# 1/rms of three norms on VectorE, by Newton steps from a guess, in place of GpSimd's power

## The chip, the cores and the metric

The program runs on one core of a Trainium2 chip. Times are device microseconds of one execution, from runs of the whole program; profile times count from the start of the profiled span. Five engines work side by side, each through its own queue in order: TensorE (PE, with its weight loads PEld), VectorE (DVE), ScalarE (ACT), GpSimd (POOL) and SyncE (SP, which issues most DMAs). They meet only at semaphores.

## The reference, cut to what matters

One decoder layer, 1024 tokens by 1024 features, all in fp32: two attention branches with gates, a SwiGLU block with 2816 hidden features, a gated embedding term, and a last norm. The norms the change touches are the last three:

```python
def rms_norm(x, g):
    x32 = x.astype(jnp.float32)
    y = x32 * lax.rsqrt(jnp.mean(x32 * x32, axis=-1, keepdims=True) + EPS)
    return (y * g.astype(jnp.float32)).astype(x.dtype)
...
        n2 = rms_norm(h, g_ffn[i])
        h = h + (jax.nn.silu(n2 @ w_ffn_gate[i]) * (n2 @ w_ffn_up[i])) @ w_ffn_down[i]

        e = rms_norm(p[i] @ w_ple_proj[i], g_ple[i])
        h = h + jax.nn.sigmoid(h @ w_ple_gate[i]) * e
    return rms_norm(h, g_final)
```

Each norm needs 1/sqrt(mean square + eps) for every token, 1024 numbers per norm.

## The kernel before

Activations are held transposed: features on the 128 partitions, tokens along the free axis, in halves of 512 tokens (hf). Every matmul is made of three passes (lines 135 to 137, function passes): a factor is split into a high part, rounded by a ScalarE copy (L129), and a low part, a VectorE subtraction (L130, function split); PE then adds high by high (L135), high by low (L136) and low by high (L137). In PE's queue these lie in just this order, so L137 is the first to need the low part of the weight factor.

A sum over features is a sum over partitions. For a norm the squares are added up in a tile acc, and PE multiplies that by a column of ones (L166, L903, L1287) into a few columns of a PSUM tile pm: one number per token, tokens on the partitions, 128 to a column. rstd_finish takes it from there: VectorE adds eps (L170), GpSimd raises to the power -0.5 (L171). It is called eight times:

- for the embedding's norm from embed(0) and embed(1), 4 columns each, into r_ple, which is read only near the end of the program;
- for the FFN's norm from scales (through rstd_cols), for the first half of the tokens (4 columns), then for two quarters (2 columns each), into r_ffn;
- for the last norm, 4, 2 and 2 columns, into a tile r.

To multiply by such a number along the free axis it has to be spread over partitions: spread puts the columns on diagonals (L761, VectorE, `acc<-ident,cols`), and PE multiplies by ones (L764, tile bc). Then VectorE scales the activations by bc: `normed` (L875) for the FFN's norm, L1292 for the last.

Where the FFN begins, the program writes out several things that overlap. out_group adds the branch output to the residual, a feature block at a time (PE tiles po, L933, squares L935 and L938, sums L939). embed multiplies the 256 embedding features by w_ple_proj (PE tiles pp) and stores its results to d_e (L913). The FFN itself is a Strassen-Winograd product: seven products instead of eight over 2x2 blocks. Its right factors are b1 to b7 (Bn in the code, `right`), sums of normed activation blocks: b1 and b2 need only the first half of the tokens, b5 and b6 quarter after quarter of the second half (t1_factors, t2_factors), and b7, b3 and b4 all of it (L1095 to L1101). Its left factors come from weights (raw), partly through sums on GpSimd (s1 at L989, L990, L1006, L1008), split into tiles wl. PE adds the products into PSUM tiles pP, pQ, pR. FIRST gives the order of the products for the first three units: b1 and b2 for all three, then b5, b6, b7, b3, b4.

In the program's text the order is: out_group and scales of the first half, normed, b1 and b2; out_group, scales and t1_factors of the third quarter; out_group of the last quarter; embed(0); embed(1); then the first two products of three units; then scales of the last quarter (the third call from scales), its factors, and the rest. A scheduler in the framework takes this text, estimates when each instruction could run, and writes each engine's queue in that order, honouring all data dependences and given priorities (scales has high_priority 800). The queue is then fixed.

Tiles with one tag share buffers. Tag wl has three: the acc tiles of out_group, the embedding's e tiles and the first weight factors wl all come from these three. A buffer is free when its last reader is done; for acc that is the L764 matmul, for e the column sums and the store to d_e.

cols is one tile of 64 columns on all partitions, with constants, gains, r_ple (32 to 39) and r_ffn (40 to 47).

Of the kernel before, what the change touches and what calls it, by code (L numbers as in the profile page):

```python
# [12 lines left out]
I32 = mybir.dt.int32  # L13
AF = mybir.ActivationFunctionType
ALU = mybir.AluOpType
# [4 lines left out]
P = 128  # L20
# [5 lines left out]
EPS = 1e-6  # L26
# [25 lines left out]
def decoder_layer(ctx: ExitStack, tc: tile.TileContext, x, p, positions, g_mix, w_in, g_q_a, w_q_b,  # L52
                  g_kv_a, w_kv_b, w_br_mla, w_br_sb, w_out, g_ffn, w_ffn_gate, w_ffn_up, w_ffn_down,
                  w_ple_gate, w_ple_proj, g_ple, g_final, xT, pT, out):
    nc = tc.nc
# [50 lines left out]
    cols = const.tile([P, 64], F32, name="cols")  # L106
    mhalf = cols[:, 0:1]
# [47 lines left out]
    with ExitStack() as att:  # L155
# [6 lines left out]
        def rstd_cols(acc, out_r, n=4):  # L162

            pt = ps.tile([P, HALF], F32, name="pm", **M)
            for i in range(n):
                nc.tensor.matmul(pt[:, i:i + 1], lhsT=acc[:, i * P:(i + 1) * P], rhs=ones, start=True, stop=True)  # L166
            rstd_finish(pt, out_r, n)

        def rstd_finish(pt, out_r, n=4):
            nc.vector.tensor_scalar(out=out_r, in0=pt[:, 0:n], scalar1=EPS, scalar2=None, op0=ALU.add)  # L170
            nc.gpsimd.tensor_tensor(out=out_r, in0=out_r, in1=mhalf.broadcast_to([P, n]), op=ALU.pow)  # L171

        with ExitStack() as sb:
            nx = ExitStack()
# [108 lines left out]
            with ExitStack() as p2:  # L283
# [21 lines left out]
                V = nc.vector  # L305
# [174 lines left out]
            for pr in range(HEADS // 2):  # L480
                kst, q1, q2 = cur
                oT = wp.tile([P, S], F32, name="oT", tag="oT", bufs=1)
                for a in range(2):
# [5 lines left out]
                                            op=ALU.subtract)  # L489
# [28 lines left out]
        with ExitStack() as ml:  # L518
# [30 lines left out]
            for c in range(2):  # L549
                nc.vector.scalar_tensor_tensor(out=cn[c], in0=cn[c], scalar=gcol[:, 3 + c:4 + c], in1=rs,  # L550
                                               op0=ALU.mult, op1=ALU.mult)
# [32 lines left out]
            for c in range(3):  # L584
                t = wk.tile([P, S], F32, name="cq", tag="pw1", bufs=4)
                with tc.issue_after(fence[0]):
# [3 lines left out]
                                               op0=ALU.mult, op1=ALU.subtract)  # L590
# [306 lines left out]
    def embed(hf):  # L897
        pt = ps.tile([P, HALF], F32, name="pm", **B)
        es = []

        def column_sums(f):
            for i in range(4):
                nc.tensor.matmul(pt[:, i:i + 1], lhsT=es[f][:, 1, i * P:(i + 1) * P], rhs=ones, start=f + i == 0,  # L903
                                 stop=f == 7, skip_group_check=True)

        for f in range(NK):
            fs = slice(f * P, (f + 1) * P)
            pp = ps.tile([P, HALF], F32, name="pp", **A)
            passes(pp, [((wpj[:, 0, k, fs], wpj[:, 1, k, fs]), (pw[hf][:, 0, k, :], pw[hf][:, 1, k, :])) for k in range(2)])
            e = wk.tile([P, 2, HALF], F32, name="e", tag="wl", bufs=3)  # L910
            nc.scalar.copy(out=e[:, 0, :], in_=pp)
            nc.scalar.activation(out=e[:, 1, :], in_=pp, func=AF.Square, scale=1.0 / 32.0)
            nc.sync.dma_start(out=d_e[fs, hcol(hf)], in_=e[:, 0, :])  # L913
            es.append(e)
            if f:
                column_sums(f - 1)
        column_sums(7)
        rstd_finish(pt, r_ple[:, 4 * hf:4 * hf + 4])
# [267 lines left out]
    for i in (1, 2, 6, 5, 7, 3, 4):  # L1186
# [31 lines left out]
        f, t = {1: (0, 0), 2: (0, 0), 6: (0, 1), 5: (1, 1), 7: (1, 1), 3: (0, 1), 4: (1, 0)}[i]  # L1218
# [23 lines left out]
    for hf, c0, n in ((1, 0, 4), (0, 0, 2), (0, 2, 2)):  # L1242
# [4 lines left out]
        if hf == 0 and en is None:  # L1247
# [5 lines left out]
            for f in range(NK):  # L1253
                nc.vector.scalar_tensor_tensor(out=en[:, f, :], in0=en[:, f, :], scalar=gains[:, 1, f:f + 1], in1=bc[0],
                                               op0=ALU.mult, op1=ALU.mult)
        for f in range(NK):
# [5 lines left out]
            if hf:  # L1262
# [3 lines left out]
                                               op0=ALU.mult, op1=ALU.mult)  # L1266
# [17 lines left out]
        pt = ps.tile([P, HALF], F32, name="pm", **M)  # L1284
        for sq in (acc[:, 0, :], sg):
            for i in range(n):
                nc.tensor.matmul(pt[:, i:i + 1], lhsT=sq[:, i * P:(i + 1) * P], rhs=ones, start=sq is not sg and i == 0,  # L1287
                                 stop=sq is sg, skip_group_check=True)
        rstd_finish(pt, r[:, 0:n], n)
        bo = spread(acc[:, 1, :], r[:, 0:n], n, B)[:, w_]  # L1290
        for f in range(NK):
            nc.vector.scalar_tensor_tensor(out=hres[:, f, s], in0=hres[:, f, s], scalar=gains[:, 2, f:f + 1], in1=bo,  # L1292
                                           op0=ALU.mult, op1=ALU.mult)
# [39 lines left out]
```

## Time and profile before

| what | value |
|---|---|
| time, three runs | 1746.61, 1748.95, 1750.78 us; median 1748.95 |
| the profiled execution | 1749.03 us, span 1747.2 us |
| busy, share of span | PE 95%, DVE 64%, ACT 50%, POOL 21% |
| calls of the power (L171) | 5 between 939.4 and 998.2 us, 3 between 1693.1 and 1737.8 us |
| embedding's products on PE | first at 950.05 us |
| first FFN product on PE | 992.95 us |

Rows of a timeline read: start in us, duration in us, engine, line, operation, tile written <- tiles read, shapes, and in brackets how long the engine was idle before and what released it. "x8" merges eight instructions that follow each other. Where merged rows of two instructions start closer than the first lasts, their ends overlap. In rows of a chain stand only start, duration and what. In a table of stretches the engines' busy times stand in the order the header names. Buffer numbers are left out of tile names in the profile.

### The profile page before, as it was taken

What the parts mean: (1) busy time and instruction counts of PE and PEld (TensorE: products, weight loads), DVE (VectorE), ACT (ScalarE), POOL (GpSimd) and SP (SyncE); (2) the same over time, 40 slices, a digit from 0 to 9 for tenths busy, and PEclk for the clock granted to TensorE, in tenths of its full rate; (3) what the DMA queues carried; (4) which work ended last, traced back from release to release, by engine and by line L of the source; (5) the groups of instructions that cost most, each with busy time, mean ns of one, the idle gap of its engine ahead of it and who ended that gap; (6) DMA issues with size and microseconds to landing.
All of it is one profiled execution on the core that took longest, in us unless ns stands there. A gap on an engine that the chain in (4) does not pass through costs nothing.

```text
span 1747.2 us, 22835 instructions
## 1 busy us (share of the span) xinstructions
PE 1665.0 (95%) x8100; PEld 1383.4 (79%) x8100; DVE 1115.2 (64%) x1874; ACT 881.3 (50%) x1740; POOL 368.6 (21%) x389
## 2 busy tenths in 40 slices
PE   6999999999987999998999899999999999999997
PEld 5887778777776788886789787877778778888787
DVE  6655785576766777686568745565666545656665
ACT  5255676576675776686325633333333334445412
POOL 2012220000021333331001733344344310000000
PEclk9999999999998999999999999999999999999998
DMA  5221222212223322124854423364564528665522
GB/s 175 59 69 37 61 57 65 67 60 67 85 85 127 104 68 86 59 70 157 284 201 153 145 78 129 126 216 151 187 197 163 199 88 316 193 193 183 170 81 74
DMA packets 167987, 222.10 MB, mean 127 GB/s; under 512 B 22914, under 2 KB 97666, under 8 KB 167874
## 3 DMA queue, kind: packets, MB, share of 16 engines
q1 hardware_dynamic: 161298, 200.21, 35.6%
q0 software_dynamic: 6032, 19.93, 3.3%
q8 instruction: 63, 1.03, 0.2%
q10 hardware_dynamic: 544, 0.52, 0.1%
q14 instruction: 50, 0.41, 0.1%
HBM read 151.93 MB, written 67.90 MB: 126 GB/s over the span
## 4 chain that ended last, share of the span: by engine, by line
PE 74%; DVE 10%; issue 6%; ACT 4%; DMA 3%; POOL 3%; SPq 0%; POOLq 0%; DVEq 0%; ACTq 0%
PE pt L135 5%; PE pt L136 4%; PE pt L137 4%; PE pd L135 4%; PE pd L136 4%; PE pd L137 4%; PE pP L137 4%; PE pP L135 4%; PE pP L136 4%; PE pg L135 2%; PE pg L136 2%; PE pg L137 2%; PE pb L135 2%; DVE T L433 2%; PE pb L137 2%
## 5 line engine op out<-in xcount | busy, mean ns | idle before, releaser
L135 PE MATMUL pt<-nTh,w_h 128*128 128x512 f32 (+1 forms) x480 | 191.7, 405 | 1.6 <-DVE e L436 1.1
L137 PE MATMUL pt<-nTh,w_l 128*128 128x512 f32 (+1 forms) x480 | 189.7, 401 | 1.6 <-DVE w_l L130 1.6
L136 PE MATMUL pt<-nTl,w_h 128*128 128x512 f32 (+1 forms) x480 | 190.8, 402 | 0.0
L130 DVE TENSOR_TENSOR wl<-raw,wl 128x512 fp32r<-128x512 f32 x132 | 109.4, 830 | 102.5 <-ACT wl L129 101.9
L129 ACT CAST wl<-raw 128x512 fp32r<-128x512 f32 x132 | 82.0, 622 | 127.6 <-PE pP L137 54.5
L137 PE MATMUL pP<-b,wl 128*128 128x512 f32 x352 | 137.2, 392 | 9.0 <-DVE wl L130 9.0
L135 PE MATMUL pP<-b,wl 128*128 128x512 f32 x352 | 138.0, 392 | 5.0 <-ACT wl L129 4.5
L136 PE MATMUL pP<-b,wl 128*128 128x512 f32 x352 | 137.7, 391 | 0.0
L135 PEld LDWEIGHTS pt<-nTh,w_h 128*128 128x128 f32 (+1 forms) x480 | 91.6, 191 | 22.5 <-DVE e L436 1.9
L137 PEld LDWEIGHTS pt<-nTh,w_l 128*128 128x128 f32 (+1 forms) x480 | 91.3, 190 | 20.9 <-DVE w_l L130 2.0
L136 PEld LDWEIGHTS pt<-nTl,w_h 128*128 128x128 f32 (+1 forms) x480 | 91.3, 190 | 18.4
L136 PE MATMUL pd<-drs,dls 128*128 128x512 f32 x296 | 101.4, 389 | 0.0
L137 PE MATMUL pd<-drs,dls 128*128 128x512 f32 x296 | 101.2, 389 | 0.0
L130 DVE TENSOR_TENSOR drs<-drr,drs 128x512 fp32r<-128x512 f32 x74 | 50.9, 690 | 75.3 <-ACT drs L129 75.3
L135 PE MATMUL pd<-drs,dls 128*128 128x512 f32 x296 | 98.7, 392 | 0.0
L129 ACT CAST drs<-drr 128x512 fp32r<-128x512 f32 x74 | 45.9, 623 | 99.5 <-PE pd L137 93.3
L430 DVE SCALAR_TENSOR_TENSOR e<-z,e 128x128 f32<-128x128 f32 (+3 forms) x96 | 51.2, 550 | 60.5 <-ACT e L429 60.2
L657 POOL TENSOR_SCALAR pw<-pw,st 128x128 f32<-128x128 f32 (+5 forms) x48 | 74.1, 1548 | 74.3 <-PE sp L639 22.3
L137 PEld LDWEIGHTS pP<-b,wl 128*128 128x128 f32 x352 | 66.2, 188 | 26.0 <-DVE wl L130 12.4
L455 DVE TENSOR_TENSOR tl<-tp,th 128x512 fp32r<-128x512 f32 (+1 forms) x96 | 50.9, 549 | 51.5 <-ACT th L454 51.4
L135 PEld LDWEIGHTS pP<-b,wl 128*128 128x128 f32 x352 | 66.5, 189 | 19.2 <-ACT wl L129 4.8
L136 PEld LDWEIGHTS pP<-b,wl 128*128 128x128 f32 x352 | 66.5, 189 | 13.9
(368 smaller groups left out, 4596.6 us busy)
## 6 DMA issues: line engine op xcount, KB each, us to landing
d_g<-t SPq DMA_DIRECT2D x74, 256.0 KB, 2.7
drr<-d_g SPq DMA_DIRECT2D x74, 256.0 KB, 3.1
w_raw<-w_in SPq DMA_DIRECT2D x33, 512.0 KB, 4.0
raw<-w_ffn_gate SPq DMA_DIRECT2D x11, 1024.0 KB, 6.3
raw<-w_ffn_up SPq DMA_DIRECT2D x11, 1024.0 KB, 6.0
spare<-w_ffn_down SPq DMA_DIRECT2D x44, 256.0 KB, 3.7
d_w<-spare SPq DMA_DIRECT2D x44, 256.0 KB, 6.1
drr<-d_w SPq DMA_DIRECT2D x44, 256.0 KB, 2.6
```

Of the source, the lines that this page charges most:

```text
L129: nc.scalar.copy(out=h, in_=src)
L130: eng.tensor_tensor(out=l, in0=src, in1=r32(h), op=ALU.subtract)
L135: nc.tensor.matmul(ps, lhsT=ah, rhs=bh, start=first and i == 0, stop=False, **kw)
L136: nc.tensor.matmul(ps, lhsT=ah, rhs=bl, start=False, stop=False, **kw)
L137: nc.tensor.matmul(ps, lhsT=al, rhs=bh, start=False, stop=last and i == n - 1, **kw)
L430: nc.vector.scalar_tensor_tensor(out=e[:, 0:w], in0=z[:, 0:w], scalar=0.0, in1=e[:, 0:w], op0=ALU.max, op1=ALU.add)
L433: nc.vector.tensor_tensor_scan(out=T[:, 0:w][:, ::-1], data0=back, data1=back, initial=carry, op0=ALU.add, op1=ALU.max)
L455: nc.vector.tensor_tensor(out=tl[:, c0:], in0=tp[:, c0:], in1=r32(th[:, c0:]), op=ALU.subtract)
L657: nc.gpsimd.tensor_scalar(out=pw[:, 0:nk], in0=pw[:, 0:nk], scalar1=st[:, 6:7], scalar2=None, op0=ALU.mult)
```

## The change

rstd_finish no longer uses GpSimd. VectorE adds eps into a scratch column group m, shifts the bits of m right by one as integers, subtracts that from 1597463007 (a first guess of 1/sqrt from the bits), and improves the guess by four Newton steps y <- y (1.5 - 0.5 m y y), each of three instructions. That makes 15 VectorE instructions where there were one on VectorE and one on GpSimd. m is cols[:, 4:4+n] and the second scratch, t, is cols[:, 56:56+n], the same columns in every call.

```diff
         def rstd_finish(pt, out_r, n=4):
-            nc.vector.tensor_scalar(out=out_r, in0=pt[:, 0:n], scalar1=EPS, scalar2=None, op0=ALU.add)
-            nc.gpsimd.tensor_tensor(out=out_r, in0=out_r, in1=mhalf.broadcast_to([P, n]), op=ALU.pow)
+
+            V = nc.vector
+            m, t = cols[:, 4:4 + n], cols[:, 56:56 + n]
+            y, yi = out_r, out_r.bitcast(I32)
+            V.tensor_scalar(out=m, in0=pt[:, 0:n], scalar1=EPS, scalar2=None, op0=ALU.add)
+            V.tensor_scalar(out=yi, in0=m.bitcast(I32), scalar1=1, scalar2=None, op0=ALU.logical_shift_right)
+            V.tensor_scalar(out=yi, in0=yi, scalar1=-1.0, scalar2=1597463007.0, op0=ALU.mult, op1=ALU.add)
+            for _ in range(4):
+                V.tensor_tensor(out=t, in0=y, in1=y, op=ALU.mult)
+                V.scalar_tensor_tensor(out=t, in0=t, scalar=-0.5, in1=m, op0=ALU.mult, op1=ALU.mult)
+                V.scalar_tensor_tensor(out=y, in0=t, scalar=1.5, in1=y, op0=ALU.add, op1=ALU.mult)
```

Lines behind it move by nine: L761 becomes L770, L875 L884, L999 L1008, L1101 L1110. The fifteen instructions are L174 to L176 and, four times, L178 to L180.

The scheduler writes other queues where the FFN begins. VectorE around the third call from scales, before (pm_9583 is that call's column sums, bc_9590 its broadcast, b5 and b6 factors of the third quarter):

```order
L130 TENSOR_TENSOR b5_8872<-t_8670,b5_8872 128x256
L130 TENSOR_TENSOR b6_8873<-spare_8713,b6_8873 128x256 x4
L170 TENSOR_SCALAR cols_85<-pm_9583 128x2
L761 TENSOR_SCALAR acc_9069<-ident_75,cols_85 128x128 x2
L875 SCALAR_TENSOR_TENSOR t_8660<-t_8660,cols_85,bc_9590 128x256
L875 SCALAR_TENSOR_TENSOR t_8664<-t_8664,cols_85,bc_9590 128x256
```

It stood ahead of both calls of the embedding's norm. And now (pm_9376 is the column sums of embed(1), pm_9635 those of the third scale; wl_9517 and wl_9538 are the first two units' first weight factors), the beginning and the end of the stretch:

```order
L174 TENSOR_SCALAR cols_85<-pm_9376 128x4
L175 TENSOR_SCALAR cols_85<-cols_85 128x4
L176 TENSOR_SCALAR cols_85<-cols_85 128x4
L178 TENSOR_TENSOR cols_85<-cols_85 128x4
L179 SCALAR_TENSOR_TENSOR cols_85<-cols_85 128x4
L180 SCALAR_TENSOR_TENSOR cols_85<-cols_85 128x4
L178 TENSOR_TENSOR cols_85<-cols_85 128x4
L130 TENSOR_TENSOR wl_9517<-raw_8656,wl_9517 128x512
L179 SCALAR_TENSOR_TENSOR cols_85<-cols_85 128x4
L130 TENSOR_TENSOR wl_9538<-raw_9374,wl_9538 128x512
L180 SCALAR_TENSOR_TENSOR cols_85<-cols_85 128x4
```

```order
L178 TENSOR_TENSOR cols_85<-cols_85 128x2
L179 SCALAR_TENSOR_TENSOR cols_85<-cols_85 128x2
L180 SCALAR_TENSOR_TENSOR cols_85<-cols_85 128x2
L770 TENSOR_SCALAR acc_9095<-ident_75,cols_85 128x128 x2
L130 TENSOR_TENSOR wl_9559<-raw_9512,wl_9559 128x512
L884 SCALAR_TENSOR_TENSOR t_8660<-t_8660,cols_85,bc_9655 128x256
L884 SCALAR_TENSOR_TENSOR t_8664<-t_8664,cols_85,bc_9655 128x256
```

The third scale has moved behind both calls of the embedding's norm, and with it the last quarter's norm and factors, behind three weight subtractions.

The end of that block of factors on VectorE, now (b7, b3 and the sums for b4, then the first weight factor that comes from a sum, wl_9737):

```order
L130 TENSOR_TENSOR b7_8887<-t_8672,b7_8887 128x512
L130 TENSOR_TENSOR b3_8888<-t_8688,b3_8888 128x512
L1110 TENSOR_TENSOR t_8674<-t_8674,spare_8713 128x512
L1110 TENSOR_TENSOR t_8678<-t_8678,spare_8713 128x512
L1110 TENSOR_TENSOR t_8682<-t_8682,spare_8713 128x512
L1110 TENSOR_TENSOR t_8686<-t_8686,spare_8713 128x512
L130 TENSOR_TENSOR wl_9737<-s1_9514,wl_9737 128x512
L130 TENSOR_TENSOR wl_9754<-s1_9535,wl_9754 128x512
```

Before, the same factor was wl_9672, and it stood behind b1 and b2's weight factors, with b7, b3 and b4 all ahead of those:

```order
L130 TENSOR_TENSOR b4_8876<-t_8686,b4_8876 128x512
L130 TENSOR_TENSOR wl_9525<-raw_8656,wl_9525 128x512
L130 TENSOR_TENSOR wl_9544<-raw_9335,wl_9544 128x512
L130 TENSOR_TENSOR wl_9564<-raw_9460,wl_9564 128x512
L999 TENSOR_TENSOR spare_8713<-pR_9529,spare_8713 128x512
L130 TENSOR_TENSOR wl_9672<-s1_9462,wl_9672 128x512
```

So the block of factors that stood ahead of the first weight factors now stands between them and the first s1 factor.

PE's queue where that factor is read, now (pQ_9740 is the first unit's product with b5, pR_9620 the third unit's with b2, pQ_9775 the third unit's with b5):

```order
L136 MATMUL pR_9620<-b2_8884,wl_9616 128x512
L137 MATMUL pR_9620<-b2_8884,wl_9616 128x512
L135 MATMUL pQ_9775<-b5_8885,wl_9772 128x512
L136 MATMUL pQ_9775<-b5_8885,wl_9772 128x512
L137 MATMUL pQ_9740<-b5_8885,wl_9737 128x512
L135 MATMUL pQ_9740<-b5_8885,wl_9737 128x512
```

Before, the same L137 into the first pQ followed directly on the third unit's product with b2; now two more units have their first two matmuls with b5 ahead of it. The third broadcast has moved too, from among the embedding's products to behind the first two units' products with b1, 24 matmuls after the FFN's first.

At the end of the program VectorE's queue has the fifteen instructions in place of the add, in one piece for the last call; PE's two earlier broadcasts of the last norm stand 21 and 30 matmuls later than before.

## The prediction

> **What bounds the kernel now.** I read the page's head first, then the group of the removed instruction, then the timeline around each place where it runs.
>
> ```profile
> PE 1665.0 (95%) x8100; PEld 1383.4 (79%) x8100; DVE 1115.2 (64%) x1874; ACT 881.3 (50%) x1740; POOL 368.6 (21%) x389
> ```
>
> TensorE (PE) is busy 95% of the span, so a microsecond is won or lost only where PE waits. The eight powers are one line, L171, and the view of that line says who waited for them:
>
> ```profile
> L171 POOL TENSOR_TENSOR cols<-cols x5: 697/1018/17272, 939.4 to 998.2; 128x4 f32<-128x4 f32 x3, 128x2 f32<-128x2 f32 x2
> L171 POOL TENSOR_TENSOR r<-r,cols x3: 695/696/1017, 1693.1 to 1737.8; 128x2 f32<-128x2 f32 x2, 128x4 f32<-128x4 f32 x1
>   DVE acc L761: 4.0, 5
> ```
>
> Two places, then: five calls near 940 to 1000 us (three scales of the FFN norm, two of the embedding's norm), and three at the end. VectorE (DVE) waited 4.0 us for them in all. PE itself waited for none of them directly. The end has nothing beside it:
>
> ```profile
> 1737.52 0.16 DVE L170 TENSOR_SCALAR r<-pm 128x2 f32<-128x2 f32 x1 [1.62 <-PE pm L1287]
> 1738.56 0.48 DVE L761 TENSOR_SCALAR acc<-ident,r 128x128 f32<-128x128 f32 x2 [0.87 <-POOL r L171]
> 1740.35 3.22 DVE L1292 SCALAR_TENSOR_TENSOR hres<-hres,cols,bc 128x256 f32<-128x256 f32 x8 [1.32 <-PE bc L764]
> ```
>
> From the add of eps (1737.52) to the diagonal (1738.56) the power path takes 1.04 us, all of it on the path.
>
> Around 985 us PE stands still. SyncE's queue and the chain of waits, in order of time, tell why:
>
> ```profile
> 984.52 0.38 SPq L860 DMA_DIRECT2D raw<-w_ffn_gate  x1
> 985.00 2.16 SPq L913 DMA_DIRECT2D d_e<-e  x3
> ```
>
> ```profile
> 985.00 7.17 DMA d_e<-e
> ...
> 992.27 0.63 ACT wl L129
> 992.95 0.80 PE pP L135
> 993.74 0.43 PE pP L136
> ...
> 995.45 0.43 PE pP L136
> 995.87 0.27 PE pP L137
> 996.38 0.23 PE pP L136
> ```
>
> The first weight factor of the FFN overwrites an embedding tile (same three buffers, tag wl) whose store was issued right behind a 1 MB weight load. Once PE restarts, its first six matmuls come 0.43 us or more apart, then 0.23: six of them take 2.92 us in place of 1.4, so a standstill costs 1.5 us on top of itself. While PE stood, VectorE did not:
>
> ```profile
> 968.04 0.16 DVE L170 TENSOR_SCALAR cols<-pm 128x2 f32<-128x2 f32 x1 [1.83 <-PE pm L166]
> 969.02 0.48 DVE L761 TENSOR_SCALAR acc<-ident,cols 128x128 f32<-128x128 f32 x2 [0.82 <-POOL cols L171]
> 973.14 3.23 DVE L875 SCALAR_TENSOR_TENSOR t<-t,cols,bc 128x256 f32<-128x256 f32 x8 [3.63 <-PE bc L764]
> 991.34 1.89 DVE L130 TENSOR_TENSOR b<-t,b 128x512 fp32r<-128x512 f32 x3
> ```
>
> ```profile
> core 0: us, PE busy (x) PEld busy (x) DVE busy (x) ACT busy (x) POOL busy (x), PEclk, DMA share, GB/s
> 973.14:993.15 20.01, 15.18 (x102) 13.72 (x102) 20.01 (x44) 15.95 (x35) 16.54 (x2) 0.90 0.54 179
> ```
>
> The third scale of the FFN norm (add at 968.04) releases a block of 44 VectorE instructions that fills 973.14 to 993.15 without a gap: the last quarter's norm and the factors b3, b5, b6, b7, b4. All of it lies under the embedding's matmuls and that standstill; it is free only because it is early.
>
> **The change, part by part.** *Removed*: eight powers. The longest of them serves r_ple, which is read long after, so its end gives nothing; the 4.0 us above is the ceiling of the gain.
>
> ```profile
> 976.85 17.27 POOL L171 TENSOR_TENSOR cols<-cols 128x4 f32<-128x4 f32 x1 [3.47 <-DVE cols L170]
> ```
>
>
> *The length of one Newton chain.* Each call becomes 15 VectorE instructions, each reading what the one before wrote. The trace has such pairs, an add and the reciprocal of its result on 128x1:
>
> ```profile
> 709.14 0.16 DVE L651 TENSOR_TENSOR st<-st 128x1 f32<-128x1 f32 x1 [0.34 <-ACT pw L647]
> 709.34 0.16 DVE L653 RECIPROCAL st<-st 128x1 f32<-128x1 f32 x1
> ...
> 717.26 0.15 DVE L651 TENSOR_TENSOR st<-st 128x1 f32<-128x1 f32 x1
> 717.45 0.17 DVE L653 RECIPROCAL st<-st 128x1 f32<-128x1 f32 x1
> ```
>
> They start 0.20 and 0.19 us apart. I take 0.19: 15 x 0.19 = 2.85 us. No shift and no small scalar_tensor_tensor on such a form stands in this trace; the bounds are 0.07 us (711.21 to 711.28, two small neighbours that do not depend on each other) and 0.28 (128x128 forms of L430), and the pair is nearest.
>
> ```profile
> 711.21 0.15 DVE L651 TENSOR_TENSOR st<-st 128x1 f32<-128x1 f32 x1
> 711.28 0.55 DVE L640 TENSOR_REDUCE st<-sp 128x1 f32<-128x384 f32 x1
> L430 DVE SCALAR_TENSOR_TENSOR e<-z,e 128x128 f32<-128x128 f32 x16 | 4.5, 278 | 7.5 <-ACT e L429 7.5
> ```
>
> *The end*: 2.85 - 1.04 = **+1.8 us** (from 0 at 0.07 to +3.2 at 0.28). The two earlier calls of the final norm cost nothing: their broadcasts stand behind more matmuls now (one of them 65 where it was 35), and PE is gapless there, with VectorE busy 14.2 of 20 us.
>
> ```profile
> 1700.00:1720.00 20.00, 20.00 (x170) 20.00 (x169) 14.21 (x36) 6.26 (x18) 0.70 (x1) 1.00 0.29 107
> ```
>
>
> *The FFN transition*: here the order matters more than the durations. m and t are the same columns of cols in every call, so calls run one behind the other in the program's order; the third scale is written after both embedding norms, and its first write must wait until the second of those is finished. The order in the section on the change shows it: the third scale's diagonal and the normed quarter now stand behind the embedding, behind the first two weight subtractions and both Newton chains. Step by step, with R the time of PE's restart (992.95 before):
>
> 1. R. One of two broadcast matmuls leaves the embedding's stretch, about 0.5 us; the store behind the 1 MB load stays. R moves by **-0.5**.
> 2. From R to the quarter's norm. PE has 24 matmuls ahead of the broadcast: 2.92 for six and 18 x 0.23 = 4.15, together 7.1. VectorE starts its first subtraction at R too and has two of them (0.6 each by the row of 991.34), 20 dependent small steps at 0.19, two free ones at 0.07 and the 0.48 diagonal: 5.6. PE is later, by 1.5. With 0.5 from broadcast to norm (972.66 below to 973.14) the block starts at R + 7.6.
> 3. The block. Up to the low half of the first s1 factor (wl_9737) VectorE now has 46 instructions: 40 of the 44, without the add and three b4 (20.01 - 0.07 - 1.8 = 18.1), then three weight subtractions, two sums of L1008 and wl_9737 itself, six by 0.6 = 3.6. That is 21.7 us, so wl_9737 is there at R + 29.3.
> 4. PE. The matmul that needs it, the first L137 into pQ, ran at 1011.2, that is R + 18.25; four matmuls (0.93) are drawn ahead of it now.
>
> ```profile
> L137 PE MATMUL pQ<-b,wl x5: 389/389/389, 1011.2 to 1013.9; 128*128 128x512 f32 x5
> 972.66 0.43 PE bc L764 x2
> ```
>
> PE's queue runs in order, so it stands until R + 29.3: 29.3 - 18.25 - 0.93 = **+10.1 us**, and the slow restart adds **+1.5**. Nothing later takes the delay back, since PE has next to no idle time behind it; the emptiest stretch of 100 us is this one:
>
> ```profile
> 1200.00:1300.00 100.00, 95.86 (x420) 1.00 0.58 192
> ```
>
>
> *Shared data path of VectorE and GpSimd.* Where GpSimd runs two-input sums, VectorE's take longer:
>
> ```profile
> 1043.45 1.76 DVE L1047 TENSOR_TENSOR t<-spare,t 128x512 f32<-128x512 f32 x1 [1.18 <-POOL t L1054]
> 1043.37 1.29 POOL L989 TENSOR_TENSOR s<-raw 128x512 f32<-128x512 f32 x1
> 999.18 4.69 POOL L1006 TENSOR_TENSOR raw<-s,raw 128x512 f32<-128x512 f32 x3
> 1003.82 4.70 POOL L1008 TENSOR_TENSOR raw<-raw 128x512 f32<-128x512 f32 x3
> ```
>
> 1.76 in place of the 0.6 to 0.7 above. Two of the first units' six GpSimd sums (L1006, L1008) now come free while the Newton chains run. Bounds: none, or six by 1.07 = +6.4. I take **+1.0**: two meet the chains (2.1), of which step 2 hides 1.5, and 0.4 is kept for the gapless block, where VectorE seems to win: the 17.27 us power did not get through. The Trainium skill, SBUF — State Buffer, section "Who interferes with whom", states a rule that speaks against this change: a VectorE instruction with two SBUF inputs and a GpSimd instruction that reads SBUF lock each other out, each for a whole instruction. Twelve of the fifteen Newton steps are of that kind; the row of 1043.45 agrees. By the rule, with GpSimd first each time, it would be rival one.
>
> **Sum**: -0.5 + 10.1 + 1.5 + 1.0 + 1.8 = +13.9. The profiled execution took 1749.03 us (span 1747.2 and 1.8 around it), 0.1 above the median of 1748.95: 1749.0 + 13.9 = **1763 us**, 0.8% slower.
>
> **Rivals.** *One, the lock-out.* All six GpSimd sums get in ahead of VectorE: 6.4, less the 1.5 of step 2, in place of 1.0, so 1763 + 3.9 = 1767. For it: after L1006 began at 999.18 VectorE's subtractions stretched likewise. Against it: GpSimd starved from 976.85 to 994. Chance 0.14.
>
> *Two, the block stays hidden; not slower.* If VectorE's block were through by the time PE gets to the first L137 into pQ, only the end and the small gain ahead of R would be left: 1749.0 - 0.5 + 1.8 = 1750.3, no change. PE gets there at R + 18.25 + 0.93 + 0.5 = R + 19.7; it decides whether the 46 instructions fit into 19.7 - 7.6 = 12.1 us in place of 21.7, 0.26 us each. The mean of the 44 is 0.45, which speaks against it; for it speaks only that I read the new order's need from rows and have not seen PE stand. Chance 0.12.
>
> *Three, faster.* The store that holds R lands in the 2.1 us that is usual for the queue rather than 7.2 (rows below), and the block does stay hidden: R comes about 5 us sooner, 1750.3 - 5 = 1745. It needs the store ahead of the load; the order has the load first. Chance 0.04.
>
> ```profile
> DMA to landing us min/median/max: 2.0/2.1/7.2
> ```
>
> **How the numbers follow.** The forecast has 0.70. Its own range: 1757 (no lock-out, store 5 us sooner) to 1769 (lock-out in part, small steps at 0.28). One adds to its upper end. The range for 8 in 10 reaches from 1753 to 1769: it leaves out two and three and the tail above. This kernel's runs can tell about 0.2%, 3.5 us, from no change. Slower: forecast and one, with a bit for the rest, 0.85; the same: most of two, 0.11; faster: 0.04.
>
> **What would show it.** Right: a wait of PE of 6 to 10 us ahead of L137 into pQ, released by VectorE's wl; the quarter's norm (now L884) starting near 1000 rather than 973; 2.7 to 3.0 us from the add to the diagonal at the end; the first weight cast still held by the store of d_e until about 992. Wrong: no such wait (two); VectorE's small steps at 0.5 us and more while GpSimd runs (one); the first cast before 988 (three). A stall inside the embedding's matmuls, whose first four tiles now share one buffer because the other two still hold acc tiles, would be a cost that I put at nothing: a tile's copy (0.6, as the cast of 992.27) and store (2.1) exceed PE's time per tile (six matmuls at 0.23 and the column sums below, 2.2) by half a microsecond, three times over, which the four banks ahead of PE cover; if they don't, it costs 1.5.
>
> ```profile
> 953.49 0.79 PE pm L903 x8
> ```

## The result: 18 us slower, at the upper edge of the range

The changed kernel takes 1769.0 us (median of four runs, 1763.0 to 1770.0), the kernel before 1749.4 in four runs beside it. The ratio is 1.0106, with a 95% interval of 1.0087 to 1.0125: slower by 18.5 us (15.2 to 21.9). The forecast was 1763, so the direction was right and the size short by 4 to 5 us, and the median lies at the upper edge of the range.

The profiled execution took 1763.02 us (span 1760.6) and is the fastest of the four. That it meets the forecast to the microsecond is an accident. TensorE's first embedding product ran at 945.5 us in it and at 950.0 in the profile before; up to there the two programs hardly differ, and the other kernels below, with the same early code, begin it anywhere between 946.1 and 950.7. The length from that product to the first product of the down projection (pd) is free of such a head start. The groups of both tiles on PE, first the kernel before (from 950.0, as in the prediction's table of the time before):

```profile
L135 PE MATMUL pp<-pw,wpj x32: 387/397/577, 950.0 to 983.6; 128*128 128x512 f32 x32
L135 PE MATMUL pd<-dwl x12: 389/393/500, 1423.8 to 1435.8; 128*128 128x512 f32 x12
```

and now the changed kernel:

```profile
L135 PE MATMUL pp<-pw,wpj x32: 387/397/501, 945.5 to 979.2; 128*128 128x512 f32 x32
L135 PE MATMUL pd<-dwl x12: 389/393/500, 1435.8 to 1447.9; 128*128 128x512 f32 x12
```

473.8 us have become 490.3: the FFN costs **16.5 us** more. The end costs 1.9 more, as the timeline of VectorE shows there (the add, the shift, the diagonal that follows the last step):

```profile
1749.07 0.16 DVE L174 TENSOR_SCALAR cols<-pm 128x2 f32<-128x2 f32 x1 [1.21 <-PE pm L1296]
1749.27 0.17 DVE L175 TENSOR_SCALAR r<-cols 128x2 int32<-128x2 int32 x1
...
1752.02 0.48 DVE L770 TENSOR_SCALAR acc<-ident,r 128x128 f32<-128x128 f32 x2
```

2.95 us from add to diagonal in place of 1.04. 16.5 + 1.9 = 18.4, which is close to the 18.5 of the runs; less the head start of 4.5 it is 13.9, close to the 14.0 between the two profiled executions.

The table of waits in the FFN transition (938 to 1040 us; engine and line, what for, us in all, times, longest) names the place:

```profile
PE pQ L137 <- DVE wl L130: 6.3, 1, 6.3
PE pP L135 <- ACT wl L129: 3.2, 1, 3.2
PE pR L135 <- DVE spare L1008: 2.4, 1, 2.4
PE pQ L135 <- DVE spare L1008: 2.3, 1, 2.3
```

The new wait ahead of L137 into pQ is there, released by VectorE's weight subtraction. Two more, on the sums of L1008, stand just ahead of it. PE's restart and that L137 in the timeline:

```profile
987.22 0.80 PE L135 MATMUL pP<-b,wl 128*128 128x512 f32 x1 [3.18 <-ACT wl L129]
...
1022.77 0.80 PE L137 MATMUL pQ<-b,wl 128*128 128x512 f32 x1 [6.26 <-DVE wl L130]
```

With R = 987.22, the L137 runs at R + 35.6 where it ran at R + 18.25 before. VectorE's timeline from R on shows what lies between, and GpSimd's what ran beside it:

```profile
987.20 0.69 DVE L130 TENSOR_TENSOR wl<-raw,wl 128x512 fp32r<-128x512 f32 x1 [1.76 <-ACT wl L129]
987.81 1.24 DVE L179 SCALAR_TENSOR_TENSOR cols<-cols 128x4 f32<-128x4 f32 x1
988.97 0.68 DVE L130 TENSOR_TENSOR wl<-raw,wl 128x512 fp32r<-128x512 f32 x1
989.57 1.23 DVE L180 SCALAR_TENSOR_TENSOR cols<-cols 128x4 f32<-128x4 f32 x1
990.84 1.20 DVE L178 TENSOR_TENSOR cols<-cols 128x4 f32<-128x4 f32 x1
992.07 0.16 DVE L179 SCALAR_TENSOR_TENSOR cols<-cols 128x4 f32<-128x4 f32 x1
...
997.15 3.22 DVE L884 SCALAR_TENSOR_TENSOR t<-t,cols,bc 128x256 f32<-128x256 f32 x8 [0.26 <-PE bc L773]
...
1009.40 0.68 DVE L1008 TENSOR_TENSOR spare<-pR,spare 128x512 f32<-128x512 f32 x1
1010.00 0.89 DVE L130 TENSOR_TENSOR b<-t,b 128x256 fp32r<-128x256 f32 x1
1010.81 1.51 DVE L130 TENSOR_TENSOR b<-spare,b 128x256 fp32r<-128x256 f32 x1
1012.24 1.77 DVE L130 TENSOR_TENSOR b<-t,b 128x512 fp32r<-128x512 f32 x1
...
1015.53 4.17 DVE L130 TENSOR_TENSOR b<-t,b 128x512 fp32r<-128x512 f32 x5
...
1022.03 1.28 DVE L130 TENSOR_TENSOR wl<-s,wl 128x512 fp32r<-128x512 f32 x2
```

```profile
987.30 1.73 POOL L999 TENSOR_TENSOR raw<-raw 128x512 f32<-128x512 f32 x1
988.99 3.04 POOL L1015 TENSOR_TENSOR raw<-s,raw 128x512 f32<-128x512 f32 x2
...
1001.45 12.01 POOL L1017 TENSOR_TENSOR raw<-raw 128x512 f32<-128x512 f32 x3 [3.12 <-DVE wl L130]
```

The block that the third scale releases begins at 997.15 (R + 9.9) and lasts 24.9 us to the start of the low half wl<-s (1022.03), 25.6 to its end. Three Newton steps of 128x4 take 1.2 us in place of 0.16 while GpSimd runs L999 and L1015. Later the factor subtractions take 0.89, 1.51 and 1.77 where 0.42 and 0.69 are usual.

### The profile page after: what moved, and what is told of

The parts are those of the page before. It is cut to its first block, busy times and chain, and to the rows that moved or that the text cites. A ratio compares the mean times of both kernels' runs of the same rounds, so it can differ in the third digit from the quotient of the medians.

```text
span 1760.6 us, 22924 instructions
## 1 busy us (share of the span) xinstructions
PE 1666.7 (95%) x8100; PEld 1382.6 (79%) x8100; DVE 1137.7 (65%) x1986; ACT 882.0 (50%) x1740; POOL 350.7 (20%) x381
## 4 chain that ended last, share of the span: by engine, by line
PE 73%; DVE 11%; issue 6%; ACT 4%; DMA 3%; POOL 3%; SPq 0%; DVEq 0%; POOLq 0%; ACTq 0%
PE pt L135 5%; PE pt L136 5%; PE pt L137 5%; PE pd L135 4%; PE pd L136 4%; PE pd L137 4%; PE pP L137 4%; PE pP L135 3%; PE pP L136 3%; PE pg L135 2%; PE pg L136 2%; PE pg L137 2%; DVE t L1056 2%; PE pQ L137 2%; PE pQ L135 2%
## 5 line engine op out<-in xcount | busy, mean ns | idle before, releaser
L137 PE MATMUL pt<-nTh,w_l 128*128 128x512 f32 (+1 forms) x480 | 187.8, 397 | 1.6 <-DVE w_l L130 1.6
L137 PE MATMUL pP<-b,wl 128*128 128x512 f32 x352 | 137.8, 393 | 8.9 <-DVE wl L130 8.9
L137 PEld LDWEIGHTS pt<-nTh,w_l 128*128 128x128 f32 (+1 forms) x480 | 90.3, 188 | 20.5 <-DVE w_l L130 2.0
L137 PE MATMUL pd<-drs,dls 128*128 128x512 f32 x296 | 101.2, 389 | 0.0
L137 PEld LDWEIGHTS pP<-b,wl 128*128 128x128 f32 x352 | 66.5, 189 | 26.0 <-DVE wl L130 12.3
L136 PEld LDWEIGHTS pP<-b,wl 128*128 128x128 f32 x352 | 66.7, 189 | 14.0
```

Of the source, the lines that this page charges most:

```text
L136: nc.tensor.matmul(ps, lhsT=ah, rhs=bl, start=False, stop=False, **kw)
L137: nc.tensor.matmul(ps, lhsT=al, rhs=bh, start=False, stop=last and i == n - 1, **kw)
```

## The experiments

Two questions: is it the order (the third scale behind the embedding's two, through the shared scratch m and t), or the 75 small instructions and the lock-out by GpSimd's sums? And what is each worth? The column "FFN" is the length from the first pp to the first pd, less the 473.8 of before, read as above; "by time" is the ratio to the kernel before, applied to 1749 us. FFN comes from one profiled execution of each kernel; the kernel before and the two that hardly touch this stretch (the rows at +0.2 and -0.1) lie 0.3 us apart.

| run | FFN | by time, with interval |
|---|---|---|
| the change | +16.5 | +18.5 (15.2 to 21.9) |
| own scratch per call | +4.3 | +5.9 (3.5 to 8.4) |
| power for the embedding's scales | +3.8 | +5.2 (3.0 to 7.5) |
| power for the FFN's scales | +1.4 | +4.7 (2.8 to 6.6) |
| steps at the end alone | +0.2 | +2.3 (0.3 to 4.4) |
| one step for four | +15.8 | +14.0 (11.2 to 16.6) |
| y in PSUM | +15.9 | +19.6 (16.3 to 23.1) |
| without L1017 | +13.0 | +12.4 (9.8 to 15.0) |
| both of these | +11.9 | +13.5 (10.5 to 16.4) |
| without L1008 | +11.8 | +14.5 (9.4 to 19.6) |
| stores first, on the change | +14.1 | +15.2 (12.2 to 18.2) |
| stores first, on the kernel before | -0.1 | -0.2 (-2.1 to +1.7) |

FFN plus the 1.9 of the end agrees with the time within its interval in every row that keeps the end's 15 steps.

### Own scratch for each call

```diff
-    cols = const.tile([P, 64], F32, name="cols")
+    cols = const.tile([P, 128], F32, name="cols")
+    calls = iter(range(8))
...
-            m, t = cols[:, 4:4 + n], cols[:, 56:56 + n]
+            c = 64 + 8 * next(calls)
+            m, t = cols[:, c:c + n], cols[:, c + 4:c + 4 + n]
```

> The change with scratch columns of its own for each of the eight calls (a wider cols tile), the same 120 VectorE instructions otherwise. Theory (the shared scratch puts the third feed-forward scale behind the two embedding scales on VectorE, so that the weights' first low half comes late): the third scale is free to be issued ahead of the embedding again, the wait of about 6 us for that low half goes, and only the end's 1.9 us and up to 1 us of the quarter's norm are left: 1.5 to 4 us above the kernel before (1751 to 1753.5). Rival (the 75 small instructions as such, and GpSimd's sums that lock them out, wherever they stand): most of the loss stays, 12 to 20 us above the kernel before (1761 to 1769).

5.9 us above the kernel before: two thirds of the loss are gone with all 120 instructions still there. VectorE's timeline (line numbers are one or two higher here) has the third scale's diagonal and the quarter's norm under the embedding's products again, and what is left of the cost further down:

```profile
976.36 0.48 DVE L772 TENSOR_SCALAR acc<-ident,cols 128x128 f32<-128x128 f32 x2
...
979.00 3.22 DVE L886 SCALAR_TENSOR_TENSOR t<-t,cols,bc 128x256 f32<-128x256 f32 x8
...
1004.64 1.25 DVE L177 TENSOR_SCALAR cols<-cols 128x4 int32<-128x4 int32 x1
1005.81 0.68 DVE L131 TENSOR_TENSOR wl<-raw,wl 128x512 fp32r<-128x512 f32 x1
1006.41 1.25 DVE L178 TENSOR_SCALAR cols<-cols 128x4 int32<-128x4 int32 x1
```

The wait of 6.3 us is gone. But the expected 1.5 to 4 was short: the embedding's steps now stand between the first weights' low halves, stretched to 1.2 us, and PE waits for such halves, 2.0 us in all in this trace:

```profile
1006.54 0.50 PE L138 MATMUL pR<-b,wl 128*128 128x512 f32 x1 [0.42 <-DVE wl L131]
...
1010.55 0.50 PE L138 MATMUL pR<-b,wl 128*128 128x512 f32 x1 [1.00 <-DVE wl L131]
```

Where the rest of the 4.3 us comes from was not taken apart.

### The power back, for one kind of call

The old two lines stand ahead of the new code, for the named calls:

```diff
+            if where == "embed":     # "scale" in the second kernel, != "end" in the third
+                nc.vector.tensor_scalar(out=out_r, in0=pt[:, 0:n], scalar1=EPS, scalar2=None, op0=ALU.add)
+                nc.gpsimd.tensor_tensor(out=out_r, in0=out_r, in1=mhalf.broadcast_to([P, n]), op=ALU.pow)
+                return
```

> GpSimd's power back for the two embedding scales alone; the three feed-forward scales and the three of the end keep the 15 VectorE steps and their shared scratch. Theory (order by the shared scratch): nothing of the embedding holds the third scale on VectorE, so the feed-forward loss goes although 45 of its 75 small steps stay: 1.5 to 5 us above the kernel before (1751 to 1754.5). Rival (the small steps as such, locked out or not): with three of five calls left, about three fifths of some 17 us stay, 10 to 14 us above the kernel before.

> GpSimd's power back for the three feed-forward scales alone; the two embedding scales and the three of the end keep the 15 VectorE steps. Theory (the third scale behind the embedding's on VectorE is the loss): GpSimd takes the third scale as in the kernel before, and 1.5 to 5 us above the kernel before are left. Rival (the embedding's locked-out steps of 1.2 us, three to six of them, are the loss): most of it stays, 8 to 18 us above. Rival (GpSimd's power, starved for 17 us in the kernel before by VectorE's gapless stream, sets the time as well): below the kernel before.

> The 15 VectorE steps for the last norm's three calls alone, power for the five ahead of them. Both theories: the feed-forward start is the kernel before's, and only the last quarter's scale is on the path: 2.95 us from the add to the diagonal in place of 1.04, so 1.9 us above the kernel before (1751.3); 0 if the end is bound by something else, 1 to 3 by the spread of these runs.

+5.2, +4.7 and +2.3. Taking either side out of the chain (the embedding's two calls, or the third scale) frees the third scale from the embedding's, and either removes 13 to 14 of the 18.5 us. In both traces the third scale's diagonal stands under the embedding's products again, at 973.01 and at 969.73. The 1.4 us that the second of them keeps in the FFN need not be a cost of its steps: eight of its embedding products, from 982.28 on, start some 0.43 us apart in place of 0.23, at a granted clock of 0.50, though no wait of PE of more than 0.4 us stands ahead of them; why is open. The third of the three kernels leaves the end's 1.9 us alone. The first came out a little above its expected 1.5 to 5, still far from the rival's 10 to 14.

### One Newton step in place of four

```diff
-            for _ in range(4):
+            for _ in range(1):
```

> The change with one Newton step in place of four for all eight calls (6 instructions each in place of 15; 1/rms is then good to about 2 in 1000, so the values that hang on it are off). VectorE's order of the calls stays: the third feed-forward scale behind the two of the embedding. Theory (the order is the loss, the count matters little): 1.8 us less at the end (9 instructions of 0.195) and 2 to 3 us less ahead of the quarter's norm, which TensorE's diagonal then sets at 7.6 us behind the first low half: 13 to 16 us above the kernel before. Rival (the count of small steps is the loss): 6 of 15 of the change's 18 to 20, so 7 to 8 us above the kernel before.

+14.0, in the theory's range and not near the rival's 7 to 8: with 9 of 15 instructions gone in every call, FFN loses 0.7 us. It is the order of the calls that costs, far more than their length. The shift and the subtraction, with one SBUF operand each, get stretched here:

```profile
991.10 1.24 DVE L175 TENSOR_SCALAR cols<-cols 128x2 int32<-128x2 int32 x1
992.37 1.21 DVE L176 TENSOR_SCALAR cols<-cols 128x2 int32<-128x2 int32 x1
```

### Steps without two SBUF operands

y is held in PSUM, in spare columns of the tile of the column sums; t and m stay as they were:

```diff
-            y, yi = out_r, out_r.bitcast(I32)
+            y, yi = pt[:, 8:8 + n], pt[:, 8:8 + n].bitcast(I32)
...
-                V.tensor_tensor(out=t, in0=y, in1=y, op=ALU.mult)
-                V.scalar_tensor_tensor(out=t, in0=t, scalar=-0.5, in1=m, op0=ALU.mult, op1=ALU.mult)
-                V.scalar_tensor_tensor(out=y, in0=t, scalar=1.5, in1=y, op0=ALU.add, op1=ALU.mult)
+                V.tensor_tensor(out=t, in0=y, in1=m, op=ALU.mult)
+                V.scalar_tensor_tensor(out=t, in0=t, scalar=-0.5, in1=y, op0=ALU.mult, op1=ALU.mult)
+                V.scalar_tensor_tensor(out=out_r if i == 3 else y, in0=t, scalar=1.5, in1=y, op0=ALU.add, op1=ALU.mult)
```

> The change with the iterate y held in PSUM (the product y*m first, the same 15 steps, the same shared scratch, m and t in SBUF): no Newton step reads two operands in SBUF, and VectorE's order of the calls stays. Theory (the order sets the loss, the lock-out by GpSimd's sums adds to it): the three steps of 1.2 us ahead of the quarter's norm take about 0.2 us each again, 3 us of the loss go and 13 to 17 us stay above the kernel before (1762 to 1766). Rival (the lock-out is the loss): 0 to 6 us above the kernel before. Rival (the lock-out costs nothing, other work hides it): as the change, 18 to 21 us above.

By time this is +19.6, no gain that can be measured, and the expected 13 to 17 was missed. The trace says where the gain went. VectorE's steps beside GpSimd's two L1015 (994.29 to 997.26) are short again, and the block starts at R + 7.95 with R = 992.53:

```profile
994.80 0.15 DVE L180 SCALAR_TENSOR_TENSOR pm<-cols,pm 128x4 f32<-128x4 f32 x1
994.99 0.16 DVE L178 TENSOR_TENSOR cols<-pm,cols 128x4 f32<-128x4 f32 x1
...
1000.48 3.22 DVE L884 SCALAR_TENSOR_TENSOR t<-t,cols,bc 128x256 f32<-128x256 f32 x8 [0.69 <-PE bc L773]
```

That is 2.0 us of the 2.3 by which the change missed R + 7.6. L137 runs at R + 33.5, also 2.0 sooner, but R itself came 0.3 later after the first pp, and behind that L137 PE has ten slow matmuls in place of seven; FFN is only 0.6 shorter. The steps' lock-out is real, and taken away alone it is worth little.

The Trainium skill, SBUF — State Buffer, section "Who interferes with whom", says that a VectorE instruction with at most one SBUF input, outside the modes that use both ports, does not contend with GpSimd, and that tensor_scalar can enter such a mode. Both fit here: 0.16 us beside L1015 with y in PSUM, and 1.24 for a shift whose one operand is in SBUF.

### Without GpSimd's second difference

```diff
-            elif i == 2:
+            elif i == 2 and order is not FIRST:
                 G.tensor_tensor(out=a12, in0=a12, in1=a11, op=ALU.subtract)
```

> The change without GpSimd's second difference (L1017) in the first three weight units: left out, so the third product of these units has other weights; VectorE's and TensorE's orders stay. In the change these three instructions run on GpSimd for 12.0 us beside the quarter's block on VectorE, some of whose instructions take 0.7 to 1.1 us longer meanwhile. Theory (the lock-out stretches the block, and the block is what TensorE waits for): the block is back at some 22 us in place of 25.6, the wait of 6.3 us ahead of L137 is 3 to 4 us shorter, and the time is 14 to 16 us above the kernel before in place of the change's 18 to 20. Rival (the block's length is its count, not the lock-out): the wait stays at about 6 us and the time at the change's. Rival (the lock-out is the whole loss): 0 to 8 us above the kernel before.

+12.4, below the expected 14 to 16; FFN is 3.5 shorter, and L137 runs at R + 31.8 in place of 35.6. The block is back at 21.8 us, as the theory had it, but the wait ahead of L137 is only 1.9 shorter (4.4) where 3 to 4 were expected: the wait of 2.3 us for the second sum of L1008 is gone as well. The five factor subtractions at the block's end start 0.60 apart again:

```profile
1012.65 0.69 DVE L1008 TENSOR_TENSOR spare<-pR,spare 128x512 f32<-128x512 f32 x1
1013.25 0.42 DVE L130 TENSOR_TENSOR b<-spare,b 128x256 fp32r<-128x256 f32 x1
1013.58 3.10 DVE L130 TENSOR_TENSOR b<-t,b 128x512 fp32r<-128x512 f32 x5
```

### Both

> The edits of the two runs before it together: y of the Newton steps in PSUM, and GpSimd's second difference (L1017) left out in the first three weight units, so that neither the steps ahead of the quarter's block nor the block itself run beside GpSimd's sums; the order of the calls on VectorE is the change's. Theory (order is the main cost, lock-out the rest): the quarter's norm starts about 8 us behind the first low half and the first low half of the next unit about 29 us behind it, as the prediction's sum had them without its term for the shared path; from TensorE's first embedding product to its first down-projection product 485 us in place of the change's 490.4 and 473.7 before, with the end 12.5 to 13.5 us above the kernel before (1761). Rival (the two gains overlap, TensorE's diagonal or its slow restart takes one of them back): 487 us there, 14 to 15.5 us above. Rival (the lock-out is the whole loss): 474 to 478 us there, 2 to 6 us above.

+13.5 by time, FFN +11.9: between the theory's 485 us and the rival's 487 (it is 485.7). PE's restart and its L137, then VectorE's block:

```profile
988.91 0.79 PE L135 MATMUL pP<-b,wl 128*128 128x512 f32 x1 [3.09 <-ACT wl L129]
...
1018.43 0.50 PE L137 MATMUL pQ<-b,wl 128*128 128x512 f32 x1 [3.01 <-DVE wl L130]
```

```profile
996.55 3.22 DVE L884 SCALAR_TENSOR_TENSOR t<-t,cols,bc 128x256 f32<-128x256 f32 x8 [0.38 <-PE bc L773]
...
1017.70 1.28 DVE L130 TENSOR_TENSOR wl<-s,wl 128x512 fp32r<-128x512 f32 x2
1018.90 0.68 DVE L1008 TENSOR_TENSOR spare<-pR,spare 128x512 f32<-128x512 f32 x1
1019.50 1.18 DVE L130 TENSOR_TENSOR wl<-s,wl 128x512 fp32r<-128x512 f32 x1
```

The block starts at R + 7.6 and lasts 21.15 us, L137 runs at R + 29.5. So the order costs about 11.9 in the FFN, and the lock-out the other 16.5 - 11.9 = 4.6. Two limits belong to this split. R came 42.7 us behind the first pp here and 41.7 in the change; counted from R to the first pd the two kernels are 5.6 us apart (443.0 and 448.6). And two rows are still stretched here: the second weight subtraction (989.57, 1.70 us), whose loss PE's diagonal hides, and the third low half in the rows above (1019.50, 1.18 us).

### Without VectorE's sums out of PSUM

In the trace above GpSimd's next sum, L1063, begun at 1012.17, was through only after VectorE had run L1008, at 1018.90, and the next subtraction then took 1.18. It looked as if GpSimd gets in only where VectorE reads PSUM, as L1008 does.

```diff
-                ready(0, 0, add(1, pt))
+                ready(0, 0, s[1] if order is FIRST else add(1, pt))
```

> The change without VectorE's three sums out of PSUM (L1008, spare<-pR) in the first three units: left out, so one quarter of those units' products lacks a term; the third scale stays behind the embedding's, and GpSimd's sums stay. In the traces so far a sum of GpSimd that finds VectorE's gapless stream waits until VectorE runs an instruction that reads PSUM (L1008, or the add of eps), and the next VectorE instruction with two operands in SBUF is then the one that takes 1.1 us longer. In the change two L1008 stand in the quarter's block. Theory (GpSimd gets in only there): without them GpSimd's sums that come due inside the block end only behind it, after 10 us or more, none of the block's instructions is stretched, and the block from the norm to the first low half is 20 to 21 us long, 1.2 less for the two L1008 and 3.7 less for the stretched ones, in place of 24.9. Rival (GpSimd gets its turn in any gap of the issue): it gets in within 5 us and the block is 23 to 25 us long.

The theory held for the block. GpSimd's three L1017 and VectorE's block:

```profile
1005.52 24.04 POOL L1017 TENSOR_TENSOR raw<-raw 128x512 f32<-128x512 f32 x3 [1.86 <-DVE wl L130]
```

```profile
1001.21 3.23 DVE L884 SCALAR_TENSOR_TENSOR t<-t,cols,bc 128x256 f32<-128x256 f32 x8 [0.25 <-PE bc L773]
...
1021.16 1.90 DVE L130 TENSOR_TENSOR wl<-s,wl 128x512 fp32r<-128x512 f32 x3
```

24.0 us for three sums that take 1.3 each when alone (the first is through at 1026.6, 1.1 us behind the end of VectorE's gapless stream), and a block of 19.95 us, without a stretched row. The time, from two runs, says only that most of the loss stays. The scheduler also wrote VectorE's queue a little differently here: the three low halves stand together.

That reading PSUM is the only way in is not shown, and the change's own trace speaks against it. L999, begun at 987.30, got in behind the weight subtraction of 987.20, which has both operands in SBUF. The first L1017, begun at 1001.45, was through at 1010.60, just behind L1008, but the second and the third then took turns with factor subtractions. And L1063 got in at once at 1015.42, behind such a subtraction, where in the two traces without L1017 it waited 6.7 us for the next L1008. What decides between these is open.

### The embedding's stores ahead of the 1 MB load

```diff
-    embed(1)
-    raws[2] = gate_up_raw(2)
+    stored = embed(1)          # now returns its last store
+    with tc.issue_after(stored):
+        raws[2] = gate_up_raw(2)
```

> The kernel before with one order changed on SP's queue: the 1 MB load of the third weight unit (L860) is issued behind the last three embedding stores (L913) in place of ahead of them. In the kernel before, that load is issued at 984.52 us when the last embedding product frees its buffer, the stores stand behind it, and TensorE stands from 984.1 to 992.95 us for the first weight cast, whose buffer such a store frees. Theory (the store behind the load holds the first weight cast; the same standstill is in the changed kernel): the first weights come 2 to 6 us earlier, the third unit's load 1.5 to 3 us later, 1 to 5 us below the kernel before. Rival (the shared data path or the casts of the factors set it): no change, within 2 us.

No change: 0.9999 (0.9988 to 1.0010). PE's first FFN matmul does come 4.6 us sooner after the first pp (986.23, in a trace whose first pp is at 947.9), and after four matmuls PE waits. The chain of waits there:

```profile
985.09 5.82 DMA raw<-w_ffn_gate
991.01 0.63 ACT wl L129
991.68 0.80 PE pP L135
```

The store no longer holds PE; the load itself does, since the third unit's weights are needed next and its buffer comes free only with the last embedding product. One of the two transfers has to be last, and PE stands for it. (VectorE's first low half, at 990.39 behind the quarter's block, had moved by less than 1 us too.) On the change the same edit moves R and also puts two of the three low halves of the second factors (wl<-s) ahead of most of the block:

> The change with the edit that did nothing for the kernel before: the third weight unit's 1 MB load behind the last embedding stores on SP's queue. In the change VectorE's queue is written differently by it: the low halves of the second weight factors of the first two units now stand after 15 of the block's instructions, ahead of the factors b5, b6, b7 and b4, in place of behind them; the third scale still stands behind the embedding's. Theory (TensorE waits for what stands in front on VectorE, so the place of the low halves is what counts): the first weights come 3 to 5 us sooner and the wait ahead of L137 goes or moves to a factor of the block; 6 to 13 us above the kernel before. Rival (the block as a whole has to be through before TensorE can go on, whichever half stands first): 14 to 19 us above. Rival (the late scale was never the matter): as the change, 18 to 20.

+15.2, FFN +14.1: the rival's range. The first L137 into pQ runs 10.6 us sooner after the first pp (66.7 in place of 77.3), and PE then stands for the third unit's low half, behind all of the block:

```profile
1028.37 0.80 PE L137 MATMUL pQ<-b,wl 128*128 128x512 f32 x1 [4.64 <-DVE wl L130]
```

The work on VectorE that starts late has to be done whichever half stands first. None of these kernels is faster than the kernel before.

## Why the prediction was right, and where it was short

- *The order* (step 2 to 4). Right. The shared scratch puts the third scale behind the embedding; freeing it by own scratch, or by taking either side away, removes 12 to 15 of the 16.5 us.
- *R* (step 1, -0.5). R is 41.7 us behind the first pp in the change and 42.9 before; in the other traces with this order 41.6 to 42.7. The sign is right and the store behind the load still held it (4.97 us to landing here); the size is -1.2 between these two traces and -0.2 to -1.3 with the others.
- *Block start* (step 2, R + 7.6). Measured R + 9.9, and R + 7.6 without the lock-out. The step took PE as the later of two; with three steps of 1.2 us VectorE was, and PE waited 1.4 us for the diagonal.
- *Block* (step 3, 21.7 us, low half at R + 29.3). The 21.7 include the low half itself: 25.6 us measured, 21.8 without the lock-out, with L137 then at R + 29.5. The count of 46 instructions and their durations was good to 0.2 us.
- *PE* (step 4, +10.1 and +1.5). The wait ahead of L137 is 6.3, at the low end of the stated 6 to 10, because PE also stands 2.4 and 2.3 us for sums of L1008 that sit in the same block; the step drew the whole delay at one place. As a sum it works out all the same. L137 runs at R + 35.6 in place of R + 18.25 + 0.93, so 16.4 later; with R's -1.2 that leaves 1.3 of the 16.5 for slow restarts, forecast as 1.5. Where the block is as forecast, without the lock-out, FFN is +11.9, and -0.5 + 10.1 + 1.5 make 11.1.
- *Shared data path* (+1.0). **This is the term that was mis-sized: 4.6 by the length from the first pp, 5.6 counted from R.** Ahead of the block three steps lose 1.05 each. In it four factor rows lose 0.47, 1.09, 1.08 and (in the row of five, 4.17 for 3.10) 1.07, together 3.7. The choice near the lower bound rested on "VectorE seems to win" in a gapless block, read from the 17.27 us of the power. That reading was right for the block of before, which reads no PSUM between the power's release (976.61) and its end. The moved block contains two L1008: the first L1017 gets in at the first of them, the other two sums follow it in turn, and L1063, which L1008 releases, gets in behind the second. Without those two reads nothing got in.
- *End* (+1.8). 1.9: the 15 steps at 0.195 to 0.20, as the pair of add and reciprocal had it.
- *No cost inside the embedding*. Right: first to last pp row 33.7 us, 33.6 before.

Rival one, the lock-out, gave 4.9 us over the order and that is about what it cost, so the likeliest case and rival one share the result. Its sign, small steps at 0.5 us and more while GpSimd runs, was seen three times (1.2 us). It was given too small a chance, and that its price fits is in part luck: it counted six sums at 1.07 less 1.5 hidden, and the trace has seven stretched rows, 6.9 us together, of which 0.9 is hidden (the three steps lose 3.15, and the block starts 2.3 late). Rivals two and three fell with the wait of 6.3 us. The median of 1769.0 is at the upper end of the range, which had been drawn to allow for part of the lock-out; the sum itself, +13.9, was 4.6 short of the measured +18.5.

## What to carry to other kernels

Scratch columns shared by several calls are an order: look at which call is now behind which on the engine's queue before costing the instructions themselves. Count the work that becomes late, all of it, and not only the instruction that is waited for. When a gapless VectorE stretch is said to shut GpSimd out, look for an instruction in it that reads PSUM, as L1008 does here.

## What was not expected of the hardware

- In these traces every GpSimd sum or power that a gapless VectorE stream kept waiting for 5 us or more got through at a VectorE instruction that reads PSUM (L1008 at 1009.40 in the change, the add of eps at 999.55 with own scratch, at 993.15 in the kernel before) or where VectorE paused (24.0 us for three sums without L1008). Sums that waited half a microsecond or less got in beside SBUF operands too, and what decides is open.
- A VectorE instruction that loses a whole turn to such a sum takes about 1.1 us more, whatever its size: 128x4 (0.16 to 1.24) as much as 128x512 (0.69 to 1.77).
- Small VectorE instructions with a single SBUF operand (the shift and subtraction on int32) are stretched in the same way, to 1.2 us.
- Dependent VectorE steps of 128x4 start 0.195 us apart with operands in SBUF, and 0.195 apart with one of them in PSUM.
